# Gate and up of a SwiGLU layer by a seven-product block scheme, with down as a stage of its own

## The chip, the cores and the metric

The kernel runs on one core of a Trainium2 chip. The core's engines work side by side, each through its own list of instructions in order: TensorE (PE; its weight loads are listed apart as PEld), VectorE (DVE), ScalarE (ACT), GpSimd (POOL) and SyncE (SP), whose list issues the DMA transfers. They wait for one another by semaphores. The metric is the device time of one launch in microseconds (us); the median of several runs is quoted, and one further run, with a profile, gives the trace.

## The reference

One decoder layer is computed for 1024 prompt tokens and 64 sample tokens (T = 1088 rows), with D = 1024 and an inner width of DFF = 2816 = 22 blocks of 128. Two mixing branches (a chunkwise mLSTM and a sliding-window attention) are merged by gates; this part is untouched. Then, in fp32:

```
x  = x + mixed @ w_out                          # 1088x1024 @ 1024x1024
h  = rms_norm(x, norm_ffn_w)
y  = x + (silu(h @ w_gate) * (h @ w_up)) @ w_down   # 1024 -> 2816 -> 1024
```

## The kernel before

Each fp32 operand `v` is split into a high part of reduced precision and a low part that holds the rest (`split`: ACT copies into `hi`, L110, DVE subtracts into `lo`, L113). A product is then three matmuls, hi·hi, hi·lo and lo·hi (`product`, L152 to L154), added up in PSUM. Sample rows, with hi and lo of 64 tokens side by side in one tile of 128, take two (`product_sample`, L159 and L160), and their halves are then added (`fold_sample`, L164 ACT and L165 DVE). The activations are held feature-major: `XH` and `XL` are [128 features, 8 blocks, 1088 tokens].

The program is written in one order, and a scheduler then moves instructions within it by its own estimates; what it settled on is fixed when the kernel is built, and each engine takes its list in order. Around the change:

- **w_out.** `TILES` is eight tiles of 128 prompt tokens and the sample tile `NCT`. For each column block `u` of 256, `by_token` multiplies a tile by w_out (24 matmuls of 256 columns) and L1038 adds the result to `X2`, the residual rows, which stay in SBUF. The loop goes over `us` = (0,), (1,), (2, 3). In its last pass each finished tile is normalised: `norm_scale` squares it on ACT with a running sum (L218), `rsqrt` makes the scale in small DVE operations (L196 to L204), `norm_apply` multiplies (L225), and `rows_to_x` turns the tile by eight TensorE transposes (L232) and splits it into XH and XL (L242 ACT, L243 DVE). The turned tile `xt2` has two buffers.
- **gate and up.** `gate_up(f)` takes block `f` of w_gate and w_up and goes over the tokens in three chunks of 384, 352 and 352 columns (`by_feature`): 24 matmuls for `pg` and 24 for `pu` in each, 144 for an `f`. ACT takes the silu, DVE multiplies and splits into `ah` and `al`, which stay in SBUF.
- **down.** After every two `f`, `down` multiplies all tiles by those two row blocks of w_down (512 columns a matmul, PSUM tile `ad`) and L1087 adds into `X2`. The matmuls of `down` for two blocks and those of `gate_up` for the next ones lie next to each other, so one can run while the other waits. In the last pass the rows are stored.

## Time and profile before

| | |
|---|---|
| median of 3 runs | 1571.07 us (1570.09 to 1571.61) |
| profiled execution, its own time | 1571.52 us |
| its span, first to last instruction | 1569.4 us |
| TensorE busy | 1538.4 us, 98% of the span |
| VectorE, ScalarE, GpSimd busy | 670.9, 400.1, 131.6 us |
| w_out from its last pass on | 724.40 to 780.33 us |
| gate, up and down | 780.33 to 1565.70 us |

Times of the trace count from the span's start. A matmul's recorded duration is its way through the array and overlaps that of the next one; what a matmul costs in a dense stretch is the distance between the starts of neighbours.

### The profile page before, as it was taken

Reading aid. Unit: us, or ns where it says so; the run is one execution under the profiler, and the core shown is the slowest. Engines: PE = TensorE matmul, PEld = TensorE weight load, DVE = VectorE, ACT = ScalarE, POOL = GpSimd, SP = SyncE. Lnnn points to the kernel's source line nnn. Section 1 sums busy time; section 2 is a strip of 40 time slices with the busy share of each in tenths; the row PEclk is TensorE's granted clock in tenths of the full one; section 3 lists DMA queues with packets and bytes.
Section 4 is the critical chain, followed back from the end, with each engine's and each line's share of the span. In section 5 each row is a group of like instructions: output and inputs, shape, how many; then the busy total and the mean of one; then the engine's idle time right before and its main releaser. Section 6 shows DMA issues by size and latency. Waiting matters only on the chain.

```text
span 1569.4 us, 23157 instructions
## 1 busy us (share of the span) xinstructions
PE 1538.4 (98%) x9686; PEld 1450.9 (92%) x9686; DVE 670.9 (43%) x1410; ACT 400.1 (25%) x854; POOL 131.6 (8%) x313
## 2 busy tenths in 40 slices
PE   6999999999999999999999999999999999999999
PEld 5887799889999999999999999998989999998987
DVE  5877524576211321244743433334343424334343
ACT  5656432323111211132331212121212112021210
POOL 0211100344000011100000000000000000000000
PEclk9999999999999999999999999999999999999999
DMA  7100122102211111151031111010211102020103
GB/s 241 47 15 17 43 71 72 48 21 58 68 41 41 41 50 45 41 181 55 1 94 41 54 41 54 28 54 4 78 54 49 33 27 81 14 68 28 41 0 114
DMA packets 106174, 84.54 MB, mean 54 GB/s; under 512 B 6290, under 2 KB 98386, under 8 KB 106070
## 3 DMA queue, kind: packets, MB, share of 16 engines
q1 hardware_dynamic: 106070, 83.07, 17.5%
q8 instruction: 76, 1.25, 0.3%
q14 instruction: 28, 0.23, 0.0%
HBM read 76.21 MB, written 6.84 MB: 53 GB/s over the span
## 4 chain that ended last, share of the span: by engine, by line
PE 92%; ACT 3%; DVE 2%; DMA 1%; issue 1%; SPq 0%; POOL 0%; ACTq 0%; DVEq 0%; POOLq 0%
PE pg L152 10%; PE pg L154 10%; PE pg L153 10%; PE acc L152 6%; PE pu L152 6%; PE pu L154 6%; PE pu L153 6%; PE acc L153 5%; PE acc L154 5%; PE ad L153 5%; PE ad L154 5%; PE ad L152 5%; PE pb L152 2%; PE pb L154 2%; PE pb L153 2%; PE po L451 1%
## 5 line engine op out<-in xcount | busy, mean ns | idle before, releaser
L152 PE MATMUL pg<-XH,wh 128*128 128x352 f32 (+1 forms) x912 | 298.5, 327 | 0.5 <-ACT th L911 0.5
L154 PE MATMUL pg<-XH,wl 128*128 128x352 f32 (+1 forms) x912 | 298.3, 327 | 0.0
L153 PE MATMUL pg<-XL,wh 128*128 128x352 f32 (+1 forms) x912 | 297.8, 327 | 0.0
L113 DVE TENSOR_TENSOR wl<-raw,wh 128x1024 fp32r<-128x1024 f32 (+1 forms) x112 | 138.0, 1243 | 182.0 <-ACT wh L110 177.2
L152 PE MATMUL acc<-wh,XH 128*128 128x256 f32 (+1 forms) x640 | 183.8, 287 | 1.1 <-ACT va L324 1.1
L154 PE MATMUL acc<-wh,XL 128*128 128x256 f32 (+1 forms) x640 | 181.3, 284 | 0.0
L153 PE MATMUL acc<-wl,XH 128*128 128x256 f32 (+1 forms) x640 | 181.3, 283 | 0.0
L1087 DVE TENSOR_TENSOR X<-ad,X 128x512 f32<-128x512 f32 x176 | 121.2, 691 | 136.7 <-PE ad L154 136.7
L153 PEld LDWEIGHTS pg<-XL,wh 128*128 128x128 f32 x912 | 171.9, 188 | 2.3
L152 PEld LDWEIGHTS pg<-XH,wh 128*128 128x128 f32 x912 | 171.3, 188 | 2.9 <-ACT th L911 0.7
L154 PEld LDWEIGHTS pg<-XH,wl 128*128 128x128 f32 x912 | 171.1, 188 | 1.5
L152 PE MATMUL pu<-XH,wh 128*128 128x352 f32 (+1 forms) x528 | 172.5, 327 | 0.0
L110 ACT CAST wh<-raw 128x1024 fp32r<-128x1024 f32 (+1 forms) x112 | 115.8, 1048 | 221.5 <-PE pg L153 111.1
L154 PE MATMUL pu<-XH,wl 128*128 128x352 f32 (+1 forms) x528 | 172.2, 326 | 0.0
L153 PE MATMUL pu<-XL,wh 128*128 128x352 f32 (+1 forms) x528 | 172.1, 326 | 0.0
L154 PE MATMUL ad<-wh,al 128*128 128x512 f32 x352 | 137.8, 391 | 0.0
L153 PE MATMUL ad<-wl,ah 128*128 128x512 f32 x352 | 137.7, 391 | 0.0
L152 PE MATMUL ad<-wh,ah 128*128 128x512 f32 x352 | 137.5, 391 | 0.0
L1064 DVE TENSOR_TENSOR sg<-sg,pu 128x352 f32<-128x352 f32 (+1 forms) x66 | 35.1, 532 | 226.0 <-PE pu L154 225.7
L152 PEld LDWEIGHTS acc<-wh,XH 128*128 128x128 f32 x640 | 122.4, 191 | 5.8 <-issue 3.9
L153 PEld LDWEIGHTS acc<-wl,XH 128*128 128x128 f32 x640 | 122.4, 191 | 0.0
L154 PEld LDWEIGHTS acc<-wh,XL 128*128 128x128 f32 x640 | 122.4, 191 | 0.0
(287 smaller groups left out, 2296.8 us busy)
## 6 DMA issues: line engine op xcount, KB each, us to landing
raw<-in_w_in_dram SPq DMA_DIRECT2D x30, 512.0 KB
raw<-in_w_gate_dram SPq DMA_DIRECT2D x22, 512.0 KB
raw<-in_w_up_dram SPq DMA_DIRECT2D x22, 512.0 KB
raw<-in_w_down_dram SPq DMA_DIRECT2D x22, 512.0 KB
xt<-in_x_prompt_dram SPq DMA_DIRECT2D x8, 512.0 KB
raw<-in_w_out_dram SPq DMA_DIRECT2D x8, 512.0 KB
X<-in_x_prompt_dram SPq DMA_DIRECT2D x8, 512.0 KB
out_dram<-X SPq DMA_DIRECT2D x16, 256.0 KB
```

Of the source, the lines that this page charges most:

```text
L110: ins = S.copy(hi, raw)
L113: V.tensor_tensor(lo, raw, f32(hi), op=ALU.subtract)
L152: PE.matmul(out, lh, rh, start=(a == 0), stop=False)
L153: PE.matmul(out, lh, rl, start=False, stop=False)
L154: PE.matmul(out, ll, rh, start=False, stop=(a == n - 1))
L451: PE.matmul(po[64 * kv:64 * kv + 64, 2 * gp:2 * gp + 2, :], z[:, 64 * kv:64 * kv + 64], pts[kv][:, 2 * blk:2 * blk + 2, :], start=(blk == ...
L1064: V.tensor_tensor(sg[:, :cn], sg[:, :cn], pu[:, :cn], op=ALU.mult)
L1087: V.tensor_tensor(X2[:nt, t, cs], r, X2[:nt, t, cs], op=ALU.add)
```

## The change

The tokens are dealt into two halves of 544: the first holds prompt tiles 0 to 3 and 32 sample tokens, the second the rest. The contraction is halved into feature blocks 0 to 3 and 4 to 7, and gate and up are the two columns of the right-hand side. Four half-by-half blocks times two by two blocks would be eight products; the new code makes seven, from sums and differences of blocks (Strassen's scheme in the variant with shared sums). On the left, `combine` makes `s1` to `s4` once (DVE L1057 to L1060, hi on ACT L1063, lo on GpSimd L1064) into `SH`, `SL` and a part of XH, XL. On the right, `right_sides` makes seven 512x128 operands for each `f` (two differences on DVE, two on GpSimd, seven splits). Each product is 4 contraction blocks by 3 matmuls by 2 halves of 272 columns (L1163): 168 matmuls of 272 columns for an `f`. Results are added up in four PSUM tiles of two banks by DVE (L1195 to L1205), and the activations go to DRAM (`AD`, `ADS`).

The residual rows go through DRAM too (`X2D`). In the last pass of w_out the tiles come in the order 0, 4, 1, 5, 2, 6, NCT, 3, 7, so that a tile and its partner are together for `combine`; the normalised tile `xn` has one buffer, the row tile `x2` three. Down becomes a stage of its own after the last `f`: for each 512-column half of w_down, groups of token tiles load their activations from DRAM (`load_act`, at most 12 blocks at a time), split them, and run all 22 blocks in one PSUM accumulation. The count of its matmuls of 512 columns stays 1144. The matmuls of w_out stay as they are.

```diff
+HALF = T // 2
+LEAD = 6
...
-    x2p, close_x2p = opened("x2p", side="right")
-    X2 = x2p.tile([P, nT, D], F32, name="X2")
...
+    X2D = ffd.tile([T, D], F32, name="X2D")
+    AD = ffd.tile([NCT, P, NF, P], F32, name="AD")
+    ADS = ffd.tile([P, NF, NB * NS], F32, name="ADS")
+    np_, close_np = opened("np", side="right")
...
+    SH = sp.tile([P, 3, 4, HALF], F32R, name="SH")
+    SL = sp.tile([P, 3, 4, HALF], F32R, name="SL")
+    acc, close_acc = opened("accD", bufs=4, space=PSUM)
+    ptp, close_ptp = opened("ptD", bufs=4, space=PSUM)
...
+    for u in range(2):
+        wu = load_cols(i["w_out"], 256 * u, 256)
+        for t, r0, nt in TILES:
+            xs = np_.tile([P, 256], F32, tag="xs", name="xs", bufs=4)[:nt]
+            nc.sync.dma_start(xs, x_rows(r0, nt)[:, 256 * u:256 * u + 256])
+            V.tensor_tensor(xs, by_token(np_, acc, col(t), nt, wu, 256), xs, op=ALU.add)
+            nc.sync.dma_start(X2D[r0:r0 + nt, 256 * u:256 * u + 256], xs)
...
+    def combine(a, b, c, n):
+        c1, c2 = slice(c, c + n), slice(HALF + c, HALF + c + n)
+        split(XH[:, 4:8, c2], XL[:, 4:8, c2], b[1])
+        s1, s2, s3, s4 = (np_.tile([P, 4, P], F32, tag=f"s{x}", name=f"s{x}")[:, :, :n] for x in range(1, 5))
+        a21 = np_.tile([P, 4, P], F32, tag="a21", name="a21")[:, :, :n]
+        S.copy(a21, b[0])
+        V.tensor_tensor(s1, b[1], a21, op=ALU.add)
+        V.tensor_tensor(s2, s1, a[0], op=ALU.subtract)
+        V.tensor_tensor(s3, a[0], a21, op=ALU.subtract)
+        V.tensor_tensor(s4, a[1], s2, op=ALU.subtract)
+        for x, hi, lo in ((s1, XH[:, 0:4, c2], XL[:, 0:4, c2]), (s2, SH[:, 0, :, c1], SL[:, 0, :, c1]),
+                          (s3, SH[:, 1, :, c1], SL[:, 1, :, c1]), (s4, SH[:, 2, :, c1], SL[:, 2, :, c1])):
+            S.copy(hi, x)
+            G.tensor_tensor(lo, x, f32(hi), op=ALU.subtract)
+
+    def arrive(t, xn, nt):
+        tps = turn_rows(ptp, xn, nt)
+        if nt == P and t >= 4:
+            combine(held.pop(t - 4), tps, t * P - 4 * P, P)
+            return
+        c, n = (t * P, P) if nt == P else (4 * P, 32)
+        for q in range(2):
+            split(XH[:, 4 * q:4 * q + 4, c:c + n], XL[:, 4 * q:4 * q + 4, c:c + n], tps[q][:, :, 0:n])
+        if nt == P:
+            held[t] = tps
+        else:
+            combine([tp[:, :, 0:32] for tp in tps], [tp[:, :, 32:64] for tp in tps], c, n)
...
+    wu = [load_cols(i["w_out"], 256 * u, 256) for u in (2, 3)]
+    raws = {0: load_f(0)}
...
-    for us in ((0,), (1,), (2, 3)):
-        wu = [load_cols(i["w_out"], 256 * u, 256) for u in us]
-        if 3 in us:
-            first = load_gate_up(0)
-        for t, r0, nt in TILES:
-            for u, ws in zip(us, wu):
-                a = by_token(np_, acc, r0, nt, ws, 256)
-                xs = X2[:nt, t, 256 * u:256 * u + 256]
-                V.tensor_tensor(xs, a, xs, op=ALU.add)
-            if 3 in us:
-                xt = np_.tile([P, D], F32, tag="xt2", name="xt2")
-                norm_apply(X2[:, t], xt, nfw, nt, norm_scale(np_, X2[:, t], nt, xt, seed=False))
-                if pending:
-                    rows_to_x(ptp, *pending)
-                pending = (xt, r0, nt)
-    rows_to_x(ptp, *pending)
-    unpack_sample()
+    for t in (0, 4, 1, 5, 2, 6, NCT, 3, 7):
+        _, r0, nt = TILES[t]
+        x2 = np_.tile([P, D], F32, tag="x2", name="x2", bufs=3)
+        nc.sync.dma_start(x2[:nt, 0:512], X2D[r0:r0 + nt, 0:512])
+        nc.sync.dma_start(x2[:nt, 512:D], x_rows(r0, nt)[:, 512:D])
+        for u, ws in zip((2, 3), wu):
+            xs = x2[:nt, 256 * u:256 * u + 256]
+            V.tensor_tensor(xs, by_token(np_, acc, col(t), nt, ws, 256), xs, op=ALU.add)
+        nc.sync.dma_start(X2D[r0:r0 + nt, 512:D], x2[:nt, 512:D])
+        xn = np_.tile([P, D], F32, tag="xn", name="xn")
+        y = norm_scale(np_, x2, nt, xn, seed=False)
+        if pending:
+            arrive(*pending)
+        norm_apply(x2, xn, nfw, nt, y)
+        pending = (t, xn, nt)
+    arrive(*pending)
...
+    left = [(XH[:, q0, first], XL[:, q0, first]), (XH[:, q1, first], XL[:, q1, first]),
+            (XH[:, q0, second], XL[:, q0, second])]
+    left += [(SH[:, n], SL[:, n]) for n in range(2)]
+    left += [(XH[:, q1, second], XL[:, q1, second]), (SH[:, 2], SL[:, 2])]
...
+    def right_sides(f):
+        g, u = raws.pop(f)
+        b11, b21, b12, b22 = (r[:, 4 * q:4 * q + 4].rearrange("p k n -> p (k n)") for r in (g, u) for q in range(2))
+        yield right(b11)
+        yield right(b21)
+        V.tensor_tensor(b11, b12, b11, op=ALU.subtract)
+        yield right(b11)
+        V.tensor_tensor(b11, b22, b11, op=ALU.subtract)
+        yield right(b11)
+        G.tensor_tensor(b12, b22, b12, op=ALU.subtract)
+        yield right(b12)
+        G.tensor_tensor(b21, b21, b11, op=ALU.subtract)
+        yield right(b21)
+        yield right(b22)
...
+    def times(out, n, w, fresh, half):
+        lh, ll = left[n]
+        for k in range(4):
+            wh, wl = w[:, k * P:k * P + P], w[:, 512 + k * P:512 + k * P + P]
+            xh, xl = (x[:, k, C * half:C * half + C] for x in (lh, ll))
+            for a, (l, r) in enumerate(((wh, xh), (wh, xl), (wl, xh))):
+                PE.matmul(out[:, half, 0:C], l, r, start=fresh and k == 0 and a == 0, stop=k == 3 and a == 2,
+                          skip_group_check=True)
...
+    def store_act(f, h, a):
+        nc.sync.dma_start(AD[4 * h:4 * h + 4, :, f, :].rearrange("t p c -> p t c"),
+                          a[:, 0:4 * P].rearrange("p (t c) -> p t c", t=4))
+        nc.sync.dma_start(ADS[:, f, 32 * h:32 * h + 32], a[:, 4 * P:HALF])
...
+    for f in range(NF):
+        outs = {}
+        w1, w2, w3, sg = (fp.tile([P, HALF], F32, tag=n, name=n) for n in ("w1", "w2", "w3", "sg"))
...
             for half in range(2):
...
+                times(outs[bank], n, w, fresh, half)
+                if n == 0:
+                    S.copy(two(w1[:])[:, half], out[:, half])
+            if n == 1:
+                S.activation(two(sg[:]), out, AF.Silu)
+            elif n == 3:
+                V.tensor_tensor(two(w1[:]), out, two(w1[:]), op=ALU.add)
+            elif n == 4:
+                V.tensor_tensor(two(w2[:]), out, two(w1[:]), op=ALU.add)
+                V.tensor_tensor(two(w2[:]), outs["d"][:, :, 0:C], two(w2[:]), op=ALU.add)
+            elif n == 5:
+                V.tensor_tensor(two(w3[:]), out, two(w1[:]), op=ALU.add)
+                S.activation(w3[:], w3[:], AF.Silu)
+                G.tensor_tensor(w2[:], w2[:], w3[:], op=ALU.mult)
+                store_act(f, 1, w2)
+            elif n == 6:
+                V.tensor_tensor(two(w1[:]), out, two(w1[:]), op=ALU.add)
+                V.tensor_tensor(w1[:], w1[:], sg[:], op=ALU.mult)
+                store_act(f, 0, w1)
...
+    def load_act(t, nt, k0, kn):
+        raw = kp.tile([P, 12, P], F32, tag="kraw", name="kraw", bufs=2)[:, :kn, :nt]
+        nc.sync.dma_start(raw, AD[t, :, k0:k0 + kn] if nt == P else ADS[:, k0:k0 + kn])
+        hi = kp.tile([P, 12, P], F32R, tag="kh", name="kh")[:, :kn]
+        if nt < P:
+            split(hi[:, :, 0:nt], hi[:, :, nt:P], raw)
+            return hi, None
+        lo = kp.tile([P, 12, P], F32R, tag="kl", name="kl")[:, :kn]
+        split(hi, lo, raw)
+        return hi, lo
...
+    for half in range(2):
+        cs = slice(512 * half, 512 * half + 512)
+        wd = load_down(half)
+        for group in ((0, 1), (NCT,), (2, 3), (4, 5), (6, 7)) if half == 0 else ((0, 1), (2, 3), (4, 5), (6, 7), (NCT,)):
+            x2s, accs = [], []
+            for t in group:
+                _, r0, nt = TILES[t]
+                x2s.append(kp.tile([P, 512], F32, tag="x2d", name="x2d", bufs=3))
+                nc.sync.dma_start(x2s[-1][:nt], X2D[r0:r0 + nt, cs])
+                accs.append(ad.tile([P, 512], F32, tag="ad", name="ad"))
+            for k0, kn in KS:
+                for t, x2, a in zip(group, x2s, accs):
+                    _, r0, nt = TILES[t]
+                    hi, lo = load_act(t, nt, k0, kn)
+                    for k in range(kn):
+                        wh, wl = wd[k0 + k]
+                        one, end = k0 + k == 0, k0 + k == NF - 1
+                        PE.matmul(a[:], hi[:, k], wh, start=one, stop=False)
+                        PE.matmul(a[:], hi[:, k], wl, start=False, stop=end and nt < P)
+                        if nt == P:
+                            PE.matmul(a[:], lo[:, k], wh, start=False, stop=end)
+                    if k0:
+                        r = a[:] if nt == P else fold_sample(kp, a, 512)
+                        V.tensor_tensor(x2[:nt], r, x2[:nt], op=ALU.add)
+                        nc.sync.dma_start(o["y_prompt"][r0:r0 + nt, cs] if r0 < SEQ else o["y_sample"][:, cs], x2[:nt])
```

How the lists of the engines read, at the places the prediction speaks of. First TensorE's list of the kernel before at two places: in the last pass of w_out, and inside the products of the first `f` (`acc` is a PSUM tile of w_out, `tp` that of four transposes, `xt2` a normalised tile, `pu` the up product).

```order
L153 MATMUL acc_7739<-wl_7476,XH_67 128x256
L232 MATMUL tp_7725<-ident_70,xt2_7625 128x128 x4
L154 MATMUL acc_7739<-wh_7475,XL_68 128x256
L152 MATMUL acc_7765<-wh_7481,XH_67 128x256
L232 MATMUL tp_7730<-ident_70,xt2_7625 128x128 x4
L153 MATMUL acc_7765<-wl_7482,XH_67 128x256
```

```order
L152 MATMUL pu_8294<-XH_67,wh_7499 128x384
L232 MATMUL tp_8213<-ident_70,xt2_8123 128x128 x4
L232 MATMUL tp_8218<-ident_70,xt2_8123 128x128 x4
L153 MATMUL pu_8294<-XL_68,wh_7499 128x384
```

The same engine after the change, from the last matmul of w_out to the first of gate and up (`xn` is the normalised tile; 7963 is that of token tile 2, then 6, NCT, 3 and 7; `pf` is a product's PSUM tile).

```order
L162 MATMUL acc_8326<-wh_7548,XL_82 128x256
L240 MATMUL tp_8082<-ident_70,xn_7963 128x128 x4
L240 MATMUL tp_8087<-ident_70,xn_7963 128x128 x4
L240 MATMUL tp_8159<-ident_70,xn_8066 128x128 x4
L240 MATMUL tp_8164<-ident_70,xn_8066 128x128 x4
L240 MATMUL tp_8262<-ident_70,xn_8143 128x64 x4
L240 MATMUL tp_8267<-ident_70,xn_8143 128x64 x4
L240 MATMUL tp_8369<-ident_70,xn_8246 128x128 x4
L240 MATMUL tp_8374<-ident_70,xn_8246 128x128 x4
L240 MATMUL tp_8384<-ident_70,xn_8353 128x128 x4
L240 MATMUL tp_8389<-ident_70,xn_8353 128x128 x4
L1163 MATMUL pf_8456<-XH_81,wh_8434 128x272
```

Before, transposes stand between matmuls of w_out or of gate and up; now those of the last five tiles stand together, with no matmul between them.

VectorE's list, before, between the normalisations of the last two prompt-side tiles (`XL<-tp` is the low part of a turned tile, `nry` a scale in the making):

```order
L243 TENSOR_TENSOR XL_68<-tp_8140,XH_67 128x4x128
L204 TENSOR_SCALAR nry_8127<-nra_8128,nry_8127 128x1
L243 TENSOR_TENSOR XL_68<-tp_8145,XH_67 128x4x128
L225 SCALAR_TENSOR_TENSOR xt2_8123<-X2_6941,nry_8127,nfw_6979 128x1024
L196 TENSOR_SCALAR nrt_8199<-nss_8197 64x1
```

and after, between those of tiles 6 and NCT (`a21` is a copy of a turned block):

```order
L233 SCALAR_TENSOR_TENSOR xn_8066<-x2_8010,nry_8070,nfw_6989 128x1024
L1101 TENSOR_TENSOR x2_8297<-acc_8300,x2_8297 128x256
L1101 TENSOR_TENSOR x2_8297<-acc_8326,x2_8297 128x256
L204 TENSOR_SCALAR nrt_8146<-nss_8144 64x1
L206 TENSOR_SCALAR nry_8147<-nrt_8146 64x1
L121 TENSOR_TENSOR XL_82<-tp_8164,XH_81 128x4x128
L207 TENSOR_SCALAR nry_8147<-nry_8147 64x1
L1057 TENSOR_TENSOR s1_8171<-tp_8164,a21_8175 128x512
L211 TENSOR_SCALAR nra_8148<-nry_8147,nrt_8146 64x1
L1058 TENSOR_TENSOR s2_8172<-s1_8171,tp_8082 128x512
L1059 TENSOR_TENSOR s3_8173<-tp_8082,a21_8175 128x512
```

The sums of a finished pair now stand between a tile's scale operations, ahead of its L233.

SyncE's list, before, in the loop over `f`, holds weight loads alone:

```order
L123 DMA raw_9129<-in_w_down_dram 128x1024
L123 DMA raw_9135<-in_w_down_dram 128x1024
L123 DMA raw_9141<-in_w_gate_dram 128x8x128
L123 DMA raw_9147<-in_w_up_dram 128x8x128
```

and after, at the end of the last `f` (`w1`, `w2` are its activations, `raw` blocks of w_down, `kraw` activations read back):

```order
L1167 DMA AD_6954<-w2_13065 128x4x128
L1169 DMA ADS_6955<-w2_13065 128x32
L131 DMA raw_13306<-in_w_down_dram 128x2x512
L1167 DMA AD_6954<-w1_13064 128x4x128
L1169 DMA ADS_6955<-w1_13064 128x32
L131 DMA raw_13312<-in_w_down_dram 128x2x512
L1245 DMA x2d_13342<-X2D_6953 128x512
L1245 DMA x2d_13345<-X2D_6953 128x512
L1228 DMA kraw_13348<-AD_6954 128x1536
```

The load that down's first matmul needs now stands behind the last store, two loads of residual rows and a load of weights.

## Rows read from the trace of the kernel before

**Rows 1.** The page: busy time of each engine; the chain that ended last.
```profile
PE 1538.4 (98%) x9686; PEld 1450.9 (92%) x9686; DVE 670.9 (43%) x1410; ACT 400.1 (25%) x854; POOL 131.6 (8%) x313
...
PE 92%; ACT 3%; DVE 2%; DMA 1%; issue 1%; SPq 0%; POOL 0%; ACTq 0%; DVEq 0%; POOLq 0%
```

**Rows 2.** Windows: stretch, length, busy by engine (PE, PEld, DVE, ACT, POOL), TensorE clock.
```profile
724.40:780.33 55.93, 55.93 (x474) 55.93 (x473) 41.69 (x114) 20.28 (x36) 1.70 (x8) 1.00 0.13 39
780.33:1565.70 785.37, 785.30 (x4331) 737.52 (x4329) 302.50 (x437) 143.49 (x227) 22.30 (x47) 1.00 0.15 47
1565.70:1569.40 3.70, 0.00 (x0) 0.00 (x0) 0.66 (x1) 0.00 (x0) 0.00 (x0) 0.96 0.38 142
```

**Rows 3.** The same, of down's PSUM tile `ad` alone (PE, PEld, DVE, ACT).
```profile
780.33:1565.70 785.37, 276.05 (x1144) 213.69 (x1144) 135.44 (x198) 12.84 (x22) 1.00 0.15 47
```

**Rows 4.** Timeline of TensorE (start, duration): ends of dense stretches, four widths.
```profile
196.33 0.28 PE L154 MATMUL acc<-wh,XL 128*128 128x264 f32 x1
...
201.89 0.29 PE L159 MATMUL acc<-wh,XS 128*128 128x264 f32 x1
...
699.83 0.28 PE L152 MATMUL acc<-wh,XH 128*128 128x256 f32 x1
...
711.35 0.28 PE L152 MATMUL acc<-wh,XH 128*128 128x256 f32 x1
...
781.47 0.33 PE L152 MATMUL pg<-XH,wh 128*128 128x384 f32 x1
...
786.66 0.34 PE L152 MATMUL pu<-XH,wh 128*128 128x384 f32 x1
...
1555.72 0.39 PE L154 MATMUL ad<-wh,al 128*128 128x512 f32 x1
...
1565.24 0.39 PE L154 MATMUL ad<-wh,al 128*128 128x512 f32 x1
```

**Rows 5.** Timeline of the norm of one tile in w_out's last pass.
```profile
753.41 0.38 PE L232 MATMUL tp<-ident,xt 128*128 128x128 f32 x2
...
763.18 1.06 ACT L218 ACTIVATE xt<-X 128x1024 f32<-128x1024 f32 x1 [2.68 <-DVE X L1038]
...
764.36 0.15 DVE L196 TENSOR_SCALAR nrt<-nss 128x1 f32<-128x1 f32 x1
...
767.24 1.28 DVE L225 SCALAR_TENSOR_TENSOR xt<-X,nry,nfw 128x1024 f32<-128x1024 f32 x1
```

**Rows 6.** Transposes inside the first gate and up products (timeline, x8 in a row).
```profile
786.84 1.04 PE L232 MATMUL tp<-ident,xt 128*128 128x128 f32 x8
```

**Rows 7.** Groups of instructions: count, busy us, mean ns; idle before.
```profile
L243 DVE TENSOR_TENSOR XL<-tp,XH 128x512 fp32r<-128x512 f32 x32 | 21.3, 684 | 5.1 <-ACT XH L242 5.1
...
L787 POOL TENSOR_TENSOR VE<-VE,mnw 128x512 f32<-128x512 f32 x8 | 9.6, 1196 | 16.4 <-DVE VE L786 15.4 <-PE acc L154 1.1
```

**Rows 8.** Timeline: two equal DVE splits, without and beside a GpSimd operation.
```profile
567.10 1.23 DVE L113 TENSOR_TENSOR wl<-raw,wh 128x1024 fp32r<-128x1024 f32 x1 [4.14 <-ACT wh L110]
...
568.83 0.95 POOL L989 TENSOR_TENSOR MIX<-MIX,gth 128x352 f32<-128x352 f32 x1 [4.86 <-DVE gth L988]
...
569.00 1.86 DVE L113 TENSOR_TENSOR wl<-raw,wh 128x1024 fp32r<-128x1024 f32 x1 [0.25 <-ACT wh L110]
```

**Rows 9.** TensorE early in the program: timeline.
```profile
11.20 0.42 PE L160 MATMUL acc<-kvl,XS 128*128 128x256 f32 x1
...
14.18 0.41 PE L160 MATMUL acc<-kvl,XS 128*128 128x256 f32 x1
```

**Rows 10.** Windows there, columns as in rows 2.
```profile
20.00:25.00 5.00, 2.87 (x17) 2.71 (x16) 3.24 (x9) 2.88 (x7) 0.39 (x1) 0.79 0.24 55
```

**Rows 11.** Timeline: a weight load of 512 KB, its issue, and the copy that waits for it.
```profile
801.14 0.38 SPq L123 DMA_DIRECT2D raw<-in_w_gate_dram  x1
...
804.78 1.05 ACT L110 CAST wh<-raw 128x1024 fp32r<-128x1024 f32 x1 [1.94 <-DMA raw<-in_w_gate_dram]
```

**Rows 12.** Timeline: the last addition.
```profile
1565.67 0.69 DVE L1087 TENSOR_TENSOR X<-ad,X 128x512 f32<-128x512 f32 x1 [0.67 <-PE ad L154]
```

More of the change, by code (lines that the diff above doesn't have):

```diff
@@ new lines, in load_f @@
+    def load_f(f):
+        both = []
+        for w in (i["w_gate"], i["w_up"]):
+            if f % 2 == 0:
+                raw = wp.tile([P, 4 * W], F32, tag="raw", name="raw", bufs=2)
+            else:
+                raw = rw.tile([P, KD * P], F32, tag="fraw", name="fraw")
+            raw = raw[:, :KD * P].rearrange("p (k n) -> p k n", k=KD)
+            nc.sync.dma_start(raw, w_rows(w, 0, KD, f * P, P))
+            both.append(raw)
+        return both
+    wu = [load_cols(i["w_out"], 256 * u, 256) for u in (2, 3)]
@@ L1047, in hybrid_kernel @@
+    arrive(*pending)
     for c in (close_ptp, close_acc, close_np):
         c()
[L1051 removed]
+    rw, close_rw = opened("rw", bufs=2)
+    fp, close_fp = opened("fp", bufs=2, side="right")
     ag, close_ag = opened("accG", bufs=4, space=PSUM)
[L1053 to L1069 removed]
@@ L1092, in hybrid_kernel @@
-    acts, wd = {}, {}
-    second = load_gate_up(1)
-    acts[0] = gate_up(*first)
-    for f in range(0, NF, 2):
-        acts[f + 1] = gate_up(*(load_gate_up(f + 1) if f else second))
-        for n in (f, f + 1):
-            wd[n] = load_down(n)
-        if f + 2 < NF:
-            acts[f + 2] = gate_up(*load_gate_up(f + 2))
-        down((f, f + 1), acts, wd, f + 2 >= NF)
-    for c in (close_ad, close_ag, close_fp, close_w2p, close_x2p, close_rsd, close_wp, close_perm):
+    C = HALF // 2
@@ new lines, in hybrid_kernel, with right @@
+    first, second = slice(0, HALF), slice(HALF, T)
+    q0, q1 = slice(0, 4), slice(4, 8)
+    left = [(XH[:, q0, first], XL[:, q0, first]), (XH[:, q1, first], XL[:, q1, first]),
+            (XH[:, q0, second], XL[:, q0, second])]
+    left += [(SH[:, n], SL[:, n]) for n in range(2)]
+    left += [(XH[:, q1, second], XL[:, q1, second]), (SH[:, 2], SL[:, 2])]
+    nslot = [0]
+    def right(src):
+        tag = "wh" if nslot[0] % 2 == 0 else "wl"
+        nslot[0] += 1
+        w = wp.tile([P, WT], F32R, tag=tag, name=tag)
+        split(w[:, 0:512], w[:, 512:1024], src)
+        return w
@@ new lines, in all_sides @@
+    def all_sides():
+        for f in range(NF):
+            if f + 1 < NF:
+                raws[f + 1] = load_f(f + 1)
+            yield from right_sides(f)
+    sides = all_sides()
+    ready = []
+    def times(out, n, w, fresh, half):
[6 more added lines that the diff above has]
+                          skip_group_check=True)
@@ new lines, in store_act, with two @@
+    def store_act(f, h, a):
+        nc.sync.dma_start(AD[4 * h:4 * h + 4, :, f, :].rearrange("t p c -> p t c"),
+                          a[:, 0:4 * P].rearrange("p (t c) -> p t c", t=4))
+        nc.sync.dma_start(ADS[:, f, 32 * h:32 * h + 32], a[:, 4 * P:HALF])
+    def two(a):
+        return a.rearrange("p (h c) -> p h c", h=2)
+    for f in range(NF):
+        outs = {}
+        w1, w2, w3, sg = (fp.tile([P, HALF], F32, tag=n, name=n) for n in ("w1", "w2", "w3", "sg"))
+        for n, bank in enumerate("aadbccd"):
+            while len(ready) < LEAD:
+                w = next(sides, None)
+                if w is None:
+                    break
+                ready.append(w)
+            fresh = bank not in outs
+            if fresh:
+                outs[bank] = ag.tile([P, 2, 512], F32, tag="ag", name="pf")
+            w = ready.pop(0)
+            out = outs[bank][:, :, 0:C]
+            for half in range(2):
+                times(outs[bank], n, w, fresh, half)
[17 more added lines that the diff above has]
+                store_act(f, 0, w1)
@@ new lines, in hybrid_kernel, with load_down @@
+    for c in (close_ag, close_fp, close_rw, close_sp, close_xp):
+        c()
+    dp, close_dp = opened("dp", bufs=12)
+    kp, close_kp = opened("kp", bufs=4, side="right")
+    ad, close_ad = opened("accD2", bufs=6, space=PSUM)
+    NG = NF // 2
+    KS = ((0, 12), (12, 10))
+    def load_down(half):
+        ws = []
+        for g in range(NG):
+            n = half * NG + g
+            ws.append(load_w([(w_rows(i["w_down"], 2 * g, 2, 512 * half, 512), 0, 512)], 2, 512,
+                             pool=wp if n < 4 else dp, htag="wh" if n < 4 else "dh", ltag="wl" if n < 4 else "dl"))
+        return [(ws[f // 2][0][:, f % 2], ws[f // 2][1][:, f % 2]) for f in range(NF)]
@@ L1103, in hybrid_kernel @@
+    for c in (close_ad, close_kp, close_dp, close_ffd, close_rsd, close_wp, close_perm):
         c()
```

83 lines of the change are left out of this document (26 added, 57 removed).

## The prediction

> **What bounds the kernel now.** I read the page first. TensorE is busy 98% of the span and 92% of the chain that ended last [rows 1]: at nearly every step it sets the pace, so the change is worth what it does to the time TensorE spends on matmuls, plus any time in which it now has none to run. The windows then give the stages. The last pass of w_out lasts from 724.40 to 780.33, and gate, up and down take 785.37 us with TensorE busy for all of it while VectorE is busy 302.50 and ScalarE 143.49 [rows 2]. The reader should see that the other engines have slack there, and that no stop exists today. Third, the timeline of dense stretches gives what a matmul costs, start to start [rows 4]: 256 columns 11.52 us in 96 intervals, 0.120; 264 columns 5.56 in 46, 0.121; 384 columns 5.19 in 30, 0.173; 512 columns 9.52 in 42, 0.2267. Each is near its columns divided by 2.4 GHz plus 11 to 14 ns; the fixed part is paid by each matmul, and the change makes matmuls more numerous and narrower.
>
> **The gate and up products.** Before: the window of 785.37 us also holds down's 1144 matmuls [rows 3], at 0.2267 [rows 4] 259.3 us, and a last group or two of transposes, of which one is 1.04 us long [rows 6], about 2.2 together. That leaves 523.9 us for 22 x 144 products. After: 22 x 168 = 3696 matmuls of 272 columns. No row has that width. The row at 264 columns, 0.121, bounds it below; 272/2.4 plus the 13.3 ns that the 512-column row carries, 0.1267, bounds it above. I take 0.1245: the 264-column row, the nearest, plus eight columns at 2.4 GHz is 0.1242. 3696 x 0.1245 = 460.2 (447 to 468). I allow 2.5 us for small frictions in the first blocks, as 523.9 contains them too (48 matmuls at 0.173 and 96 at 0.160, the latter from the same line, make 521). **Gate and up: -61 us** (-53 to -74).
>
> A rule is weighed here. The rows put the fixed part of a matmul at 11 to 14 ns [rows 4]. The Trainium skill ("TensorE: Matmul & The Clock Gate", Back-to-back issue gap) gives the columns divided by 2.4 GHz plus 2.5 ns for a matmul by itself. By it the old products would be 486.7 us, the new ones 428.0, and the gain 58.7 instead of 61; the rows of this kernel differ from it, and they decide.
>
> **Work beside the products.** For each `f` VectorE now has seven low parts and two differences of 512 columns from SBUF, each half of the 1.23 us that a split of 1024 takes [rows 8], five additions from PSUM at 544 columns (0.73 each by the 0.684 of 512 columns [rows 7]) and one product: 9.9 us of the 20.9 that TensorE needs. GpSimd has three operations of about 1.2 us [rows 7]. Both fit, and the right-hand sides are made six products, some 18 us, ahead. In the list, two products of other banks stand between a bank's last matmul and its next use, except in the last `f`, where one bank must be read before its next product: +1.5 us. The AD stores wait for nothing that TensorE needs. I cost the steady state at nothing; if that cover is gone, see the second rival.
>
> **The handover from w_out to gate and up.** Today the transposes lie between matmuls, the last of them inside gate and up [rows 6], so the norm's delay costs nothing. In the new list the transposes of the last five tiles (2, 6, NCT, 3, 7) follow the last matmul of w_out with nothing between. With matmul work unchanged, w_out would end near 777.5: 780.33 less the transposes that no longer lie before it. From then on TensorE waits for a queue of norms, and each must wait for its predecessor, because `xn` has one buffer: Square of the next tile writes the buffer that the transposes of the last one read.
>
> One link, unobstructed: from the Square's start at 763.18 to the end of the multiply, 767.24 + 1.28, is 5.34 us, with the small scale operations between (the first at 764.36), and the eight transposes take until 0.8 us after their start at 753.41 [rows 5]: 6.1 us. The new VectorE list puts more into it. After a second-half tile, a low part and the four sums, five operations of 0.684 [rows 7], stand ahead of the next multiply: 3.4 us, of which about half falls into gaps between the scale operations. Their low parts on GpSimd, four of about 1.2 us [rows 7], slow two-input VectorE operations from SBUF: a split took 1.86 us beside GpSimd against 1.23 without [rows 8]. The first link moreover carries five VectorE operations that prepare the first right-hand sides, about 3.2 us, and the x2 load of a late tile waits until an earlier tile's multiply has freed its slot; its addition is queued ahead of scale operations.
>
> So, from tile 5's transposes, which I place near 773: tile 2's multiply ends at 784 to 788 (Square 1.9 with its wait, 10.2 of VectorE work), tile 6's at 792 to 796, NCT's at 803 to 807.6 (the sums of tile 6 stand in it), tile 3's at 810.5 to 815, tile 7's at 817 to 822. With its transposes gate and up start at 818 to 823, against 780.33. **+41 us.** The ends: without any obstruction five links of 6.1 give 773 + 30.5 + 0.8 = 804.3, or +24; with every obstruction doubled about +50.
>
> **Clock.** Matmuls of 256 columns early in the program started 2.98 us apart over 14 intervals, 0.213 each [rows 9], against 0.120 [rows 4]: the level of 1.2 GHz instead of 2.4. A stretch in which TensorE was busy little over half shows a granted clock of 0.79 [rows 10]. Those 14 matmuls lost 1.3 us; the profile does not show how long a slow stretch after these two stops will be. From nothing to 3 us each, I take 2: **+4 us**. The Trainium skill says in the same page ("The HAM clock gate") that an array left idle falls to half clock, which is a rule against a change that makes two stops; no row of this kernel shows a stop of 40 us.
>
> **The handover from gate and up to down.** Today none: products of the next `f` cover it. Now the activations of the last `f` go to DRAM and back before down's first matmul can start. From the end E of the last product: an addition and a product on VectorE with splits of weights between, 2.8; two stores issued at 0.4 each [rows 11], and their landing, by then E + 5.5 to 6.7. Two residual loads and a weight load stand ahead of the load in SP's list, 0.4 each, within that time. A load of 512 KB took 3.64 us from issue to use [rows 11]; one of 768 KB at that rate 5.5, and so it lands near E + 11.5. Its copy of 1536 columns takes 1.57 (1.05 x 1.5 [rows 11]); the low part, 1.23 x 1.5 = 1.85 [rows 8], comes after it, and the third matmul needs it: E + 14.5. Below: a 5.5 us landing with the load at the rate of a small one and no splits between, 11. Above: weights and residuals ahead take the queue, 20. **+14.5 us.**
>
> **Down itself.** 1144 matmuls of 512 columns before and after: nothing. Loads of 768 KB (5.5 us) and splits (3.4 us) lie beside 8 us of matmuls for each 12 blocks, on engines that are otherwise idle; without that cover each of 36 loads would cost what it is late. **End.** The sample tile comes last, so its copy and addition, each near the 0.69 of the last addition [rows 12], stand before the final store where one did: +1.3 with the wait; the 3.70 us after the last product's addition begins [rows 2] stay.
>
> **Sum.** -61 + 1.5 + 41 + 4 + 14.5 + 1.3 = +1.3 us on a span of 1569.4 and an execution of 1571.5, which lies 0.45 above the median of the runs. Predicted median: 1572.
>
> **Rivals.** (1) *Faster: the norms are hardly obstructed.* The five links run near 6.5 us and the clock stays up: 18 us less at the first handover up to the bound of +24, 3 less at the clock, so 1551 to 1560; I name 1555. For it: most of a link is latency between small operations, into which the sums fit. Against: GpSimd and the ScalarE queue are in the same link. (2) *Slower: TensorE stalls in each `f`.* Three GpSimd operations each stretch a VectorE operation by 0.63 [rows 8], the differences form a chain from one right-hand side to the next over three engines, and results in PSUM wait behind them. At 1 us an `f` this costs 22: 1594. It decides from 0.2 us an `f` (4.4 us). Against: VectorE has 9 us to spare in each. (3) *The narrower matmul does not give the gain:* 0.1267 a matmul instead of 0.1245 is 8.1 us: 1580. For it: the 512-column row carries the larger fixed part; against: the 264-column row is the nearest in width and carries less.
>
> **How the numbers follow.** The forecast has 0.42, rival 1 0.26, rival 2 0.19, rival 3 0.13. The forecast's own range, from the ends of its handovers taken by turns, is 1562 to 1583. The range over all reaches from rival 1 to rival 2 at 0.8 us an `f`: 1553 to 1590. A measurement tells 0.2%, 3.1 us, from no change. Rival 1 and a quarter of the forecast's chance are faster: 0.37; four tenths of the forecast and little else is within 3.1 us: 0.19; the rest, with rivals 2 and 3, slower: 0.44.
>
> **What would show it.** In the profile of the changed kernel: a stop of TensorE after w_out's last matmul, broken only by ten short groups of transposes, first product near 821; starts of 272-column matmuls 0.1245 apart; 460 us plus little from the first product to the last; a second stop of 14 to 15 us, in which SP's list waits for the last store; below-full granted clock right behind both. Wrong I would be if transposes were ready at w_out's end, if the distance lay outside 0.121 to 0.127, or if TensorE had idle time in every `f`.

## The result, and the profile after

The change makes the kernel 0.7% slower: 1581.47 us (median of 4 runs, 1580.87 to 1583.0) against 1570.66 beside it, a ratio of 1.007 with a 95% interval of 1.0052 to 1.0087. The forecast was 1572 with a range of 1553 to 1590. The profiled execution has a span of 1579.8 us, 10.4 more than before.

The page of the changed kernel, busy time of each engine and the chain that ended last:

```profile
PE 1493.8 (95%) x10214; PEld 1398.1 (88%) x10214; DVE 702.3 (44%) x1417; ACT 474.4 (30%) x958; POOL 230.2 (15%) x353
...
PE 88%; DVE 5%; ACT 3%; DMA 2%; issue 1%; SPq 0%; POOL 0%; ACTq 0%; DVEq 0%; POOLq 0%
```

TensorE has 44.6 us less busy time than in [rows 1], and the kernel still takes longer: VectorE's part of the chain is 5% instead of 2, DMA's 2% instead of 1. The windows, in the columns of [rows 2], say where.

```profile
777.10:821.58 44.48, 8.55 (x40) 7.25 (x41) 32.59 (x77) 17.23 (x35) 18.77 (x18) 0.54 0.24 72
821.58:840.00 18.42, 17.13 (x126) 16.84 (x125) 9.82 (x13) 8.85 (x16) 8.03 (x6) 0.92 0.09 26
840.00:1060.00 220.00, 220.00 (x1756) 220.00 (x1756) 103.36 (x157) 63.15 (x115) 44.12 (x31) 1.00 0.27 77
...
1289.20:1303.95 14.75, 0.03 (x1) 0.00 (x0) 6.09 (x7) 3.56 (x3) 0.19 (x1) 0.61 0.87 289
1303.95:1310.00 6.05, 5.47 (x13) 3.90 (x14) 5.18 (x4) 3.67 (x4) 0.00 (x0) 0.55 0.85 229
1310.00:1440.00 130.00, 130.00 (x558) 104.39 (x558) 48.96 (x40) 36.49 (x31) 0.00 (x0) 1.00 0.54 178
```

The reader should see two stops of 44.5 and 14.8 us, a slow clock behind each, and between them a stream without gaps: 220 us for 1756 matmuls of 272 columns. Two of these began before the window, and from start to start they lie 0.1254 us apart. Down's row gives 130 us for 558 matmuls of 512 columns, 0.233 each, where 0.2267 was expected. TensorE's waits from w_out on (what it waited for, total, times, longest) name the stops:

```profile
PE tp L240 <- DVE xn L233: 35.9, 5, 8.6
PE ad L1254 <- ACT kh L118: 14.7, 1, 14.7
PE pf L1163 <- ACT SH L1063: 1.3, 1, 1.3
PE pf L1163 <- DVE w L1197: 0.8, 1, 0.8
```

The timeline of the first stop: the end of w_out, the multiplies (L233) and Squares (L226) of its norms, and the first product.

```profile
776.81 0.28 PE L162 MATMUL acc<-wh,XL 128*128 128x256 f32 x1
...
783.03 1.74 DVE L233 SCALAR_TENSOR_TENSOR xn<-x,nry,nfw 128x1024 f32<-128x1024 f32 x1
784.91 1.94 PE L240 MATMUL tp<-ident,xn 128*128 128x128 f32 x8 [7.82 <-DVE xn L233]
788.12 1.05 ACT L226 ACTIVATE xn<-x 128x1024 f32<-128x1024 f32 x1
793.37 1.28 DVE L233 SCALAR_TENSOR_TENSOR xn<-x,nry,nfw 128x1024 f32<-128x1024 f32 x1
...
803.81 1.28 DVE L233 SCALAR_TENSOR_TENSOR xn<-x,nry,nfw 64x1024 f32<-64x1024 f32 x1
...
806.41 1.06 ACT L226 ACTIVATE xn<-x 128x1024 f32<-128x1024 f32 x1 [0.21 <-PE tp L240]
810.62 1.56 DVE L233 SCALAR_TENSOR_TENSOR xn<-x,nry,nfw 128x1024 f32<-128x1024 f32 x1
...
818.56 1.28 DVE L233 SCALAR_TENSOR_TENSOR xn<-x,nry,nfw 128x1024 f32<-128x1024 f32 x1
...
821.58 0.57 PE L1163 MATMUL pf<-XH,wh 128*128 128x272 f32 x1
```

Five links, each behind the last; a Square starts only when the transposes of the tile before it are done. The transposes take 1.94 us here, in a stretch with a granted clock of 0.54, and 1.04 in [rows 6], where it was 1.00. Two of the multiplies of 128 rows ran beside GpSimd operations and took 1.74 and 1.56 instead of 1.28; the one of 64 rows at 803.81 ran beside one as well and took 1.28. The second stop, from the last product to down's first matmul:

```profile
1288.94 0.29 PE L1163 MATMUL pf<-SH,wl 128*128 128x272 f32 x1
...
1291.04 0.72 DVE L1206 TENSOR_TENSOR w<-w,sg 128x544 f32<-128x544 f32 x1
...
1291.78 0.36 SPq L1167 DMA_DIRECT2D AD<-w  x1
...
1294.41 0.91 SPq L1228 DMA_DIRECT2D kraw<-AD  x2
...
1302.43 1.47 ACT L118 CAST kh<-kraw 128x1536 fp32r<-128x1536 f32 x1 [3.30 <-DMA kraw<-AD]
...
1303.95 0.80 PE L1254 MATMUL ad<-wh,kh 128*128 128x512 f32 x1 [14.73 <-ACT kh L118]
```

And two of down's starts at the end of the program, 35 intervals apart:

```profile
1565.55 0.39 PE L1254 MATMUL ad<-dh,kh 128*128 128x512 f32 x1
...
1573.72 0.39 PE L1255 MATMUL ad<-dl,kh 128*128 128x512 f32 x1
```

8.17 us in 35 is 0.2334. In [rows 4] the same width stood 0.2267 apart.

### The profile page after: what moved, and what is told of

It is laid out like the page before. It is cut to its first block, busy times and chain, and to the rows that moved or that the text cites. A ratio compares the mean times of both kernels' runs of the same rounds, so it can differ in the third digit from the quotient of the medians.

```text
span 1579.8 us, 24924 instructions
## 1 busy us (share of the span) xinstructions
PE 1493.8 (95%) x10214; PEld 1398.1 (88%) x10214; DVE 702.3 (44%) x1417; ACT 474.4 (30%) x958; POOL 230.2 (15%) x353
## 4 chain that ended last, share of the span: by engine, by line
PE 88%; DVE 5%; ACT 3%; DMA 2%; issue 1%; SPq 1%; POOL 0%; ACTq 0%; DVEq 0%; POOLq 0%
PE pf L1163 29%; PE ad L1254 6%; PE ad L1255 6%; PE acc L160 6%; PE acc L161 5%; PE acc L162 5%; PE ad L1257 5%; PE pg L160 4%; PE pg L162 4%; PE pg L161 4%; PE pb L160 2%; PE pb L162 2%; PE pb L161 2%; PE po L459 1%; PE sc L407 1%; PE tp L240 1%
## 5 line engine op out<-in xcount | busy, mean ns | idle before, releaser
L1163 PE MATMUL pf<-XH,wh 128*128 128x272 f32 x704 | 139.6, 290 | 2.1 <-ACT SH L1063 1.3
L1163 PE MATMUL pf<-XH,wl 128*128 128x272 f32 x704 | 137.8, 288 | 0.0
L1255 PE MATMUL ad<-dl,kh 128*128 128x512 f32 x324 | 128.0, 395 | 0.0
L1254 PE MATMUL ad<-dh,kh 128*128 128x512 f32 x324 | 127.9, 395 | 0.0
L160 PE MATMUL pg<-XH,wh 128*128 128x352 f32 (+1 forms) x384 | 125.7, 327 | 0.5 <-ACT th L919 0.5
L162 PE MATMUL pg<-XH,wl 128*128 128x352 f32 (+1 forms) x384 | 125.4, 327 | 0.0
L161 PE MATMUL pg<-XL,wh 128*128 128x352 f32 (+1 forms) x384 | 125.2, 326 | 0.0
L1163 PEld LDWEIGHTS pf<-XH,wh 128*128 128x128 f32 x704 | 113.8, 190 | 2.6 <-ACT SH L1063 1.6
L1257 PE MATMUL ad<-dh,kl 128*128 128x512 f32 x288 | 113.8, 395 | 0.0
L1163 PEld LDWEIGHTS pf<-XH,wl 128*128 128x128 f32 x704 | 112.7, 188 | 0.0
L121 DVE TENSOR_TENSOR wl<-raw,wh 128x1024 fp32r<-128x1024 f32 (+1 forms) x50 | 62.8, 1264 | 104.7 <-ACT wh L118 100.0
L1163 PE MATMUL pf<-SH,wh 128*128 128x272 f32 x528 | 106.6, 288 | 0.0
L1163 PE MATMUL pf<-SH,wl 128*128 128x272 f32 x528 | 106.4, 288 | 0.0
L1163 PE MATMUL pf<-XL,wh 128*128 128x272 f32 x352 | 102.0, 290 | 0.0
L1163 PE MATMUL pf<-XL,wl 128*128 128x272 f32 x352 | 101.4, 288 | 0.0
```

The costliest lines, as they stand in the source:

```text
L121: V.tensor_tensor(lo, raw, f32(hi), op=ALU.subtract)
L160: PE.matmul(out, lh, rh, start=(a == 0), stop=False)
L161: PE.matmul(out, lh, rl, start=False, stop=False)
L162: PE.matmul(out, ll, rh, start=False, stop=(a == n - 1))
L1163: PE.matmul(out[:, half, 0:C], l, r, start=fresh and k == 0 and a == 0, stop=k == 3 and a == 2, skip_group_check=True)
L1254: PE.matmul(a[:], hi[:, k], wh, start=one, stop=False)
```

## Experiments

All are edits of the changed kernel, each timed beside the kernel before. They change the staging, the schedule or the scheme; every one computes the whole layer.

**Two buffers for the normalised tile.**

```diff
-        xn = np_.tile([P, D], F32, tag="xn", name="xn")
+        xn = np_.tile([P, D], F32, tag="xn", name="xn", bufs=2)
```

> One edit: two buffers for the normalised tile xn. Theory A, the single buffer strings the five norms in a row: the next Square and scale no longer wait for the transposes of the tile before, the stop of TensorE between w_out and the products shrinks from 44.5 us by 12 to 18, and the time falls to 1563 to 1570. Theory B, the sums on VectorE and their low parts on GpSimd fill the links by themselves: the stop shrinks by less than 4, time above 1577.

Measured: 1561.38 us, ratio 0.9937 (0.9922 to 0.9952), 20.1 us less than the changed kernel. The time from w_out's last matmul to the first product falls from 44.8 us (776.81 to 821.58) to 20.8 (779.17 to 799.92): 24 less, of which w_out's later end takes back 2.4: the transposes of two of the five tiles now lie before it. Theory A holds, with a stop that shrinks by more than the 12 to 18 it claimed. TensorE's waits there:

```profile
PE tp L240 <- DVE xn L233: 14.8, 2, 11.9
```

One wait of 11.9 us is left, for tile 3's multiply. Its timeline shows what stood between that tile's Square and the multiply:

```profile
782.70 4.87 POOL L1064 TENSOR_TENSOR SL<-s,SH 128x512 fp32r<-128x512 f32 x2 [0.20 <-ACT SH L1063]
...
783.13 1.05 ACT L226 ACTIVATE xn<-x 128x1024 f32<-128x1024 f32 x1
...
787.54 0.21 POOL L208 TENSOR_SCALAR nrt<-nrt 128x1 f32<-128x1 f32 x1
...
791.84 1.53 DVE L233 SCALAR_TENSOR_TENSOR xn<-x,nry,nfw 128x1024 f32<-128x1024 f32 x1
```

GpSimd's one small step of the scale (L208) comes right behind two low parts of sums that ended at 787.57. That suggested the next run.

**The scale off GpSimd**, with the two buffers:

```diff
-            G.tensor_scalar(t, t, -0.5, None, op0=ALU.mult)
+            (V if tag == "nr" else G).tensor_scalar(t, t, -0.5, None, op0=ALU.mult)
```

> Two buffers for xn, and the one step of the scale that ran on GpSimd (a number per row times -0.5) goes to VectorE. With two buffers alone the multiply of tile 3 came 10 us after its Square; its scale stood 1.9 us and more behind GpSimd's low parts of the sums. Theory A, that queue on GpSimd is a large part of the rest: the first stop falls by another 3 to 5, time 1556 to 1559. Theory B, VectorE's own queue (sums and first right-hand sides ahead of the multiply) sets it: change under 1.5 us, time 1560 to 1562.

Measured: 1560.88 us, ratio 0.9933 (0.9916 to 0.9949); the wait for the multiplies is 15.6 us in two, where it was 14.8. No change, as theory B said: GpSimd's queue was where the delay showed, not what set it. That VectorE's own queue sets it is the theory's reading; this run does not show it, the last one below in part.

**The scheme undone, the staging kept.** Core of the edit: eight products, no sums on either side.

```diff
-        for n, bank in enumerate("aadbccd"):
+        for n, bank in enumerate("aabbccdd"):
...
-                times(outs[bank], n, w, fresh, half)
+                times(outs[bank], 2 * (n // 4) + n % 2, now[n % 4], fresh, half)
```

> The scheme alone is undone, its staging stays: eight products of plain halves for each f (192 matmuls of 272 columns instead of 168), four right-hand sides instead of seven, no sums on either side. The products take 22 x 24 x 0.1253 = 66 us more. Theory A, the sums on the left are half of what fills the first handover: its stop shrinks by 12 to 18 and the time is 1630 to 1636. Theory B, the row of norms alone sets it: shrinks by under 4, time 1644 to 1648. If VectorE's work for the scheme held up TensorE within the f, the difference would come out under 60 with the stop unchanged.

Measured: 1635.14 us, ratio 1.041 (1.0394 to 1.0425), 53.7 more than the seven products. From first to last product 531.2 us (812.83 to 1344.04) instead of 467.4; the stop after w_out 35.6 instead of 44.8. So leaving out the eighth product is worth 64 us, near 22 x 24 x 0.1254 = 66. Its sums cost 9.2 in the first handover, together with three of its first right-hand sides, which this run leaves out too. The time lies in theory A's range, but 9.2 is less than its 12 to 18 and more than B's 4: the row of norms is the larger part, the work for the scheme the smaller.

**Activations read back early.** The first eight blocks of two tiles are loaded while the last `f` is still in its products.

```diff
+            if f == NF - 1 and n == 0:
+                early = [rw.tile([P, KD * P], F32, tag="fraw", name="fraw") for t in range(2)]
+                for t in range(2):
+                    nc.sync.dma_start(early[t][:].rearrange("p (k c) -> p k c", k=8), AD[t, :, 0:8])
```

> The first eight blocks of the first two token tiles are read back from DRAM during the last f, into two raw tiles that are free by then, ahead of the last stores in SyncE's list (down's weight tiles are 11 instead of 12 to make room). Theory A, down waits for the way of the last activations to DRAM and back, and nearly all that it needs first was stored long before: the stop falls from 14.7 us to about 3 (a copy of 1024 columns and its releases), the slow clock behind it goes too, and the time to 1567 to 1570. Theory B, what comes next is as late (the later blocks, or the weights, whose loads share the queue): the stop moves into the first 20 us of down and the time stays above 1577.

Measured: 1574.35 us, ratio 1.0021 (1.0011 to 1.003), 7.1 less. The stop is 8.0 us, not 3. Neither theory names why; the timeline does:

```profile
1291.73 1.22 DVE L121 TENSOR_TENSOR wl<-raw,wh 128x1024 fp32r<-128x1024 f32 x1
...
1292.97 0.37 SPq L131 DMA_DIRECT2D raw<-in_w_down_dram  x1
...
1296.96 1.04 ACT L118 CAST dh<-raw 128x1024 fp32r<-128x1024 f32 x1 [6.30 <-DMA raw<-in_w_down_dram]
...
1297.92 1.99 ACT L118 CAST kh<-fraw 128x1024 fp32r<-128x1024 f32 x2
...
1299.01 0.80 PE L1261 MATMUL ad<-wh,kh 128*128 128x512 f32 x1 [7.96 <-ACT kh L118]
```

The data were there, but the copy `kh` stood in ScalarE's list behind a copy of down's weights, and that one waited 6.30 us for a load that SyncE issued only at 1292.97. In SyncE's list this load stands between the two pairs of stores of the last `f`; it went out when VectorE's low part (L121) had freed the tile `raw`. A ready operation waited behind a late one. (The expectation of the next run took this for a wait on memory that the last store still held. In the built program this `kh` waits for TensorE, the last reader of the sums that lie where it goes, and not for the store; the premise was wrong.)

**The same, with down's activations laid over XH and XL**, which the products leave before their end:

```diff
-    dp, close_dp = opened("dp", bufs=11)
-    kp, close_kp = opened("kp", bufs=4, side="right")
+    kp, close_kp = opened("kp", bufs=4)
+    dp, close_dp = opened("dp", bufs=11, side="right")
```

> The early read-back, with the tiles of down's activations laid over XH and XL, which the products leave 3 us before their end, and those of its weights over the sums and the w tiles. In the run before, the copies waited until the last store had left the memory that they were to be written to. Theory A, that release was the rest of the stop: it falls from 8.0 us to under 2, little slow clock follows, time 1562 to 1566. Theory B, weights are now what is late, since their tiles wait for the last store: a stop of 3 us or more some 10 us into down, time 1568 to 1573.

Measured: 1564.68 us, ratio 0.9958 (0.9942 to 0.9975), 16.8 less than the changed kernel. The last product and down's first matmul are neighbours:

```profile
1290.31 0.29 PE L1163 MATMUL pf<-SH,wl 128*128 128x272 f32 x1
1290.44 0.39 PE L1261 MATMUL ad<-wh,kh 128*128 128x512 f32 x1
```

The time is that of theory A, for another reason than it gave: in the built program the copies wait for nothing but their load now, and stand ahead of the weights' copies in ScalarE's list. Whether the place in memory or the place in the list did it was not taken apart; the second follows from the first in this program, since the scheduler lists what it believes free. The first matmul takes 0.39 us, as at the full clock, where 0.80 stood.

**Where the operands of down begin.** The extra 7.7 us of down (1144 x 0.0067) had no row before to explain it. The matmul instructions of down are alike in both kernels but for their tiles' addresses and row lengths: in the built programs both operands of the kernel before begin at remainder 0 or 256 when divided by 512 bytes; now the weights (the moving operand, 512 columns) do, and `kh` and `kl` (the stationary operand, the 128x128 block that a weight load, PEld, brings) are at 480. The first try:

```diff
+    kp.tile([P, 8], F32, name="pad", bufs=1)
```

> One edit: 32 bytes of padding ahead of the tiles that hold down's activations, so that their rows begin at multiples of 64 bytes as all other matmul operands do (now they begin 32 bytes behind one). Theory A, the address: a matmul of down's 512 columns goes from 0.2333 us back to the 0.2267 of before, and 1144 of them give back 7.6 us: about 1574. Theory B, the form of the stage (66 matmuls into one PSUM tile, other loads beside it): the distance stays at 0.2333 and the time at 1581.

Measured: 1583.11 us, ratio 1.0078 (1.0061 to 1.0095). The pad was laid where it moved nothing: `kh` still stood at remainder 480. The run says nothing on either theory; it repeats the changed kernel, and the 1.6 us between them show by how much two such medians can differ.

```diff
+    gap, close_gap = opened("gap", side="right")
+    gap.tile([P, 120], F32, name="gap")
     kp, close_kp = opened("kp", bufs=4, side="right")
```

> The padding of the first run left the tiles where they were. Here 480 bytes are taken above them instead, and down's activations (kh, kl) begin at multiples of 512 bytes, as the matmul operands of the kernel before did at multiples of 256; nothing else changes. Theory A, the address of the stationary operand costs 6.7 ns a matmul: 0.2333 goes to 0.2267 and the time to about 1574. Theory B, something else in the stage: 0.2333 stays, time 1581 to 1583.

Measured: 1574.26 us, ratio 1.0022 (1.0012 to 1.0031), 7.2 less, as theory A said. (The gap moves the other tiles of this pool too, but no matmul reads them.) Then with `[P, 104]`, so that they begin at remainder 64:

> As the run with down's activations at multiples of 512 bytes, but with 64 bytes less taken above them, so that they begin 64 bytes behind such a multiple. Theory A, a multiple of 64 bytes is enough for the stationary operand: 0.2267 us a matmul and 1574. Theory B, a larger multiple is needed: 0.2333 and 1581 to 1583.

Measured: 1580.35 us, ratio 1.0056 (1.0041 to 1.0071), as theory B said. The window from 1380 to 1420 lies inside down in each kernel. First the aligned one (remainder 0), then remainder 64, then the run with the sides swapped, where the activations were at 0 but most of the weight tiles, `dh` and `dl`, the other operand, at 480:

```profile
1380.00:1420.00 40.00, 40.00 (x178) 33.15 (x177) 9.64 (x7) 6.99 (x5) 0.00 (x0) 1.00 0.38 128
```

```profile
1380.00:1420.00 40.00, 40.00 (x173) 32.08 (x172) 9.64 (x7) 6.96 (x5) 0.00 (x0) 1.00 0.35 125
```

```profile
1380.00:1420.00 40.00, 40.00 (x174) 32.40 (x173) 13.87 (x11) 11.06 (x9) 0.00 (x0) 1.00 0.44 145
```

178 matmuls in 40 us against 173 and 174, at the full clock in all. The run with the sides swapped holds the comparison within itself: the first eight of the 22 blocks of w_down's first half lie in `wh` and `wl`, which begin at 0 or 256, and only the others at 480. One stretch of 24 matmuls (23 intervals) of the former, one of 72 (71 intervals) of the latter:

```profile
1363.50 0.39 PE L1261 MATMUL ad<-wh,kh 128*128 128x512 f32 x1
...
1368.74 0.39 PE L1264 MATMUL ad<-wh,kl 128*128 128x512 f32 x1
...
1377.23 0.40 PE L1261 MATMUL ad<-dh,kh 128*128 128x512 f32 x1
...
1393.80 0.40 PE L1264 MATMUL ad<-dh,kl 128*128 128x512 f32 x1
```

That is 0.2278 against 0.2334, in one program, with the activations at 0 in both. So either operand at 480 costs about 6 ns, and 64 is not enough for the stationary one. Remainders of 128 were not tried in down.

**All of it.** Two buffers, the scale off GpSimd, the early read-back over XH and XL, and both operands of down at multiples of 512.

> Two buffers for xn, the scale off GpSimd, the early read-back over XH and XL, all matmul operands of down at multiples of 512 bytes. Theory A, the stops are independent and add up: from 1581.5, 20 for xn, 3 for the scale, 16 for down's start, and 7.6 if the address theory holds: 1535 to 1545, faster than both kernels. Theory B, a gain at one stop is given back at the next: above 1552.

Measured: 1538.24 us, ratio 0.9791 (0.9776 to 0.9806): 2.1% faster than the kernel before and 43 us less than the changed one. The single gains, 20.1 + 16.8 + 7.2, make 44.1, and 43.2 were measured together: the stops are independent and add up. One long wait is left, in the first handover:

```profile
PE tp L240 <- DVE xn L233: 15.6, 2, 12.6
```

**The first right-hand sides kept out of the norms**, on top of it, by loading the first block of w_up into a tile that comes free late:

```diff
-    raws = {0: load_f(0)}
+    raws = {0: load_f(0, ("w_gate",))}
...
     rw, close_rw = opened("rw", bufs=2, side="right")
+    raws[0] += load_f(0, ("w_up",), True)
```

> All changes of the best kernel, and the first block of w_up is loaded into a tile that comes free only at the end of the norms. Five of the first seven right-hand sides can then not be made among the last norms any more; VectorE's list has those 8 operations behind the last sums. Theory A, they are what keeps tile 3's multiply waiting: the first stop of 15.6 us loses 3 to 6, time 1532 to 1535. Theory B, they ran in gaps, the sums and GpSimd's low parts are what it waits for: the stop stays, or the third product now waits for its right-hand side instead, time 1538 to 1542.

Measured: 1537.72 us, ratio 0.9782 (0.9766 to 0.9798), no change. The waits:

```profile
PE tp L240 <- DVE xn L233: 9.7, 2, 6.8
PE pf L1164 <- ACT wh L118: 3.7, 1, 3.7
PE pf L1164 <- ACT w L1196: 2.8, 1, 2.8
```

Those operations did hold up the norms, by 5.9 us: the wait for the multiplies falls from 15.6 to 9.7. But the products then wait 3.7 us for a right-hand side, as in B's second branch, and 2.8 for ScalarE's copy of the first product (L1196):

```profile
801.57 0.38 SPq L1087 DMA_DIRECT2D fraw<-in_w_up_dram  x1
...
805.49 0.69 DVE L1139 TENSOR_TENSOR raw<-fraw,raw 128x512 f32<-128x512 f32 x1 [6.43 <-DMA fraw<-in_w_up_dram]
...
806.89 0.59 PE L1164 MATMUL pf<-XH,wh 128*128 128x272 f32 x1 [3.75 <-ACT wh L118]
```

The right-hand side comes late because its load, which this edit put off, was issued at 801.57; VectorE sat idle for it. Whether these operations find room behind the norms with an earlier load was not tried.

## Why the prediction was right or wrong

The two stops and their places were right, their lengths came out near, and the time lay inside the range. That the kernel is slower was hardly forecast: the sum was +1.3 us, less than the 3.1 that a measurement tells from no change, and slower had a chance of 0.44. The 9 us above 1572 need a cause.

- **Gate and up.** 0.1254 a matmul against 0.1245 forecast: 463.5 us instead of 460.2. With 1.6 us of slow clock at the start, a wait of 1.3 for the first sums and 1.0 lost at the wait in the last `f`, the stretch takes 467.4 from first to last start, 467.6 with the last matmul; forecast with the clock's 2, the friction and the last `f` were 466.2. Rival 3's price of 0.1267 was not reached. The Trainium skill's rule for a matmul by itself, columns divided by 2.4 GHz plus 2.5 ns ("TensorE: Matmul & The Clock Gate", Back-to-back issue gap), gives an estimate of 0.1158 here, and 58.5 us for the gain where the prediction wrote 58.7; the trace shows 0.1254, so the rows were the better guide.
- **Work beside the products.** From 840 to 1060 TensorE is busy 220.00 of 220 us: rival 2 did not come about, although VectorE was busy 47% of it and GpSimd 20%.
- **Handover from w_out.** Gate and up start at 821.58, forecast "near 821". The ends of the five multiplies, 784.77, 794.65, 805.09, 812.18 and 819.84, all lie in the intervals given. The run with two buffers shows the single buffer as the cause of 24 us of that stop, the run with eight products the scheme's own work as that of 9. Rival 1 asked for links near 6.5 us, with this buffer; from end to end they are 9.9, 10.4, 7.1 and 7.7. (Its 18 us down to the bound of +24 should read 17.)
- **Clock.** The windows behind the stops show granted clocks of 0.92 and 0.55. At first the products start 0.227 apart instead of 0.125, down's matmuls 0.427 instead of 0.233; this costs about 1.6 and 2.5 us, forecast 2 each.
- **Handover to down.** 14.7 us, forecast 14.5. With E at 1289.07, the load was issued at E + 5.3 (forecast 5.5 to 6.7), its copy began at E + 13.4 (forecast 11.5; weights share the queue), 1.9 late. The forecast then added a low part of 1.85, as the third matmul needs it; the first matmul started right behind the copy. The two errors nearly cancel, so that the sum met 14.7 to 0.2 is luck. What it missed is that this wait was not needed: the eight blocks that down starts with had been stored long before, and read early they leave no stop.
- **Down itself: the step that failed.** "1144 matmuls of 512 columns before and after: nothing" took the distance of [rows 4] for a property of the width. It was also one of the operands' addresses: 270.0 us from 1303.95 to one interval behind the last start, where 1144 x 0.2267 and the clock's 2 make 261.3. That is 8.7 us, 7.7 of it from 0.0067 a matmul, the rest the clock and a wait of 0.6 for the first low part; the run with the tiles at 512-byte multiples took 7.2 back.
- **Sum.** The ends of w_out, products, handover and down differ from the forecast by +0.3, +1.4, +0.2 and +8.7, the end of the program (5.9 us instead of 5.2) by +0.6: 11.2. Of these 2.2 were hidden by a slip of mine: the transposes inside the old window were left out of the products before, but not credited anywhere, as the 41 us already held their successors. 11.2 - 2.2 = 9.0, which is what the span came out above the forecast sum (10.4 against 1.3).

The scheme does what it says: 64 us in the products against eight of the same form, 9 of them lost to its sums and right-hand sides in the first handover. The products gave 56 us over those of before (467.6 against 523.9), and the staging around them, two stops, an address and the end, took 67 back. With the staging mended the kernel is 2.1% faster than before.

## What to carry to other kernels

When a change moves work off the engine that sets the pace, price the places where that engine now has nothing in its list: here two handovers of 41 and 15 us took back the 56 that the products gave, and one extra buffer and loads made early returned 37. Before blaming a transfer, look at what stands ahead of its user in that engine's list and at where its tile lies: something ready may be queued behind something late. And before a matmul's distance read from one stage is used for another, look at where the operands begin: at 512 columns the address alone was worth 7 us here.
